# Low part of the weights first in each tile, with its buffers laid out for the preceding k tile

## The chip, the cores and the metric

The kernel runs on one core of a Trainium2 chip. The metric is the device time of one execution in microseconds. The core's TensorE (PE in the profile) does matrix products, VectorE (DVE), ScalarE (ACT) and GpSimd (POOL) do elementwise work, and SyncE (SP) issues most DMA transfers.

## The reference

A two-layer block over 256 tokens and 16 learned tokens (272 positions, width 1024), batch 1, all in float32. Cut to what matters for the change:

```python
for li in range(DEPTH):                                   # 2 layers
    h = h + mixer(rms_norm(h, norm_mix_g[li]), w_in[li], w_branch[li], w_out[li], ...)
    h = h + conv_ffn(rms_norm(h, norm_ffn_g[li]), w_ffn_in[li], ..., w_ffn_out[li], valid)
return rms_norm(h, norm_final_g)[:, PAD:]

def mixer(hn, w_in, w_branch, w_out, ...):
    proj = hn @ w_in                                      # 1024 x 13312
    # retention, HGRN2 and differential attention on slices of proj
    y_b = einsum('blnc,ncd->blnd', branches, w_branch)    # three times 1024 x 1024
    return sum(sigmoid(mg) * y_b, over n) @ w_out         # 1024 x 1024

def conv_ffn(hn, w_ffn_in, conv_w, conv_b, w_ffn_out, valid):
    u = hn @ w_ffn_in                                     # 1024 x 5632
    c = conv_b + sum(conv_w[j] * shifted(u, j))           # width 3
    gate, val = split(c, 2)
    return (silu(gate) * val) @ w_ffn_out                 # 2816 x 1024
```

## The kernel before, in words

All weights are cut into 128x128 tiles, 1,616 to a layer. They stand in memory in the order in which they are used, eight tiles to a chunk (404 chunks). For each chunk one DMA on SP's queue brings 512 KB into one of three buffers `wraw`. Products are made with about float32's precision from a faster matmul type: ACT copies the chunk to `whi`, rounded to that type, and DVE subtracts to get the rest, `wlo`. There are four buffers of each, each with room for 1,152 columns, 128 more than a chunk has. The activations are split the same way, into `xh` and `xl` (the first input projections and the ffn input), or into pairs of slots such as `b0hi`, `b0lo`, `yhi`, `ylo`, `ghi`, `glo`. A slot holds four k tiles of 272 positions one behind the other, so each k tile begins 1,088 bytes after the one before, which is 4 times 256 and 64 more.

For every weight tile `run` in `products` (lines 861 to 864) issues three matmuls that add into one PSUM bank: high weights with high activations, high weights with low activations, low weights with high activations. The weights are the stationary operand, so each matmul comes with a weight load; the activations move, 272 columns in layer 0 and in six kinds of product of layer 1 (those named in `FULL`), 258 in the other products of layer 1, which leave out the first 14 positions. A product covers two blocks of 128 output features (f = 0 and 1), each in its own PSUM bank, with k on the outside and f inside: (k 0, f 0), (k 0, f 1), (k 1, f 0) and so on. The first group has four blocks, those of `hq` 0 and 1, for its first four k tiles. Two products' results fit into PSUM at a time; DVE, ACT and POOL take them out while PE does the next product.

Exceptions are the last block of layer 0's ffn output, `("fo", 3)`, which does all k of f = 0 first and then those of f = 1, and the last layer's ffn output (`final`, lines 1340 on), in which the activations are stationary and 512 columns of weights move at a time.

Where a tile lies in its `whi` and `wlo` buffer is decided by `_places` (line 121): it wants each tile at a place modulo 256 bytes that is 64 times (k modulo 4), plus 96 for the 258-column products, plus 64 for those whose activations lie in slots (`BLOCK`). `whi` and `wlo` have the same places. `_runs` (line 146) turns the places of a chunk into one access pattern of evenly spaced runs, so that one ACT and one DVE instruction split a whole chunk. `_Weights.next` (line 568) hands out the tiles, and issues a new chunk's DMA and split when it comes to one; the split is due 6 us by the planner's clock (`LEAD`) before the first use.

The order of the instructions on each engine is set by a planner (`_Plan.order`) at build time. It simulates the engines with a cost for each operation and takes, on each engine, the operation that could start first, and among equals the one with the smallest due time (`key`). The three matmuls of a tile are one operation for it. The smaller matmuls of attention, retention and HGRN2 are put between the tiles in this way. Almost every ACT, DVE and POOL instruction carries line 549, the helper that records it; it is told apart by its tiles.

Of the kernel before, what the change touches and what calls it, by code (L numbers as in the profile page):

```python
# [36 lines left out]
CHUNK_TILES = 8  # L37
# [14 lines left out]
def _pairs(name, lo, hi):  # L52
# [34 lines left out]
def _turns(li):  # L87

    pairs = [x for x in ORDER if x[0][0] not in MARKS]
    if li == DEPTH - 1:
        pairs = [x for x in pairs if x[0] != "fo"]
    groups = [[x] for x in pairs]
    if li == 0:
        groups[:2] = [pairs[:2]]
    out = []
    for group in groups:
        if group == [("fo", 3)]:
            out.append([("fo", 3, k, f) for f in range(2) for k in range(FK)])  # L100
        else:
            nk = _ktiles(group[0][0])
            out.append([x + (k, f) for k in range(nk // 2) for x in group for f in range(2)])
            out[-1] += [x + (k, f) for x in group for k in range(nk // 2, nk) for f in range(2)]
    if li == DEPTH - 1:
        out.append([("fo", j, k, f) for k in range(FK) for j in range(KD // 2) for f in range(2)])
    return out
# [2 lines left out]
STREAM = sum(2 * _ktiles(n) for n, _ in ORDER if n[0] not in MARKS)  # L110


LINE = 256
APART = (0, 96)
BLOCK = 64
ROOM = CHUNK_TILES * P + 2 * LINE // 4
T0 = META - 2
FULL = ("rk", "rv", "hf", "hi", "dk", "dv")


def _places(depth=DEPTH):

    wants = []
    for li in range(depth):
        for name, j, k, _ in sum(_turns(li), []):
            if name == "fo" and (li == DEPTH - 1 or j == 3):
                wants.append(None)
                continue  # L130
            short = li == DEPTH - 1 and name not in FULL
            wants.append(APART[short] + BLOCK * (name[0] == "b" or name in ("wo", "fo")) + 64 * (k % 4))
    out = []
    for c in range(0, len(wants), CHUNK_TILES):
        at, places = 0, []
        for want in wants[c : c + CHUNK_TILES]:
            if want is not None:
                at += (want // 4 - at) % (LINE // 4)
            places.append(at)
            at += P  # L140
        assert at <= ROOM
        out.append(places)
    return out


def _runs(places):


    runs = []
    for i, at in enumerate(places):  # L150
        if runs and at == runs[-1][1] + runs[-1][2] * P:
            runs[-1][2] += 1
        else:
            runs.append([i, at, 1])
    out = []
    for i, at, n in runs:
        if out and out[-1][4] == n and (out[-1][3] == 1 or at == out[-1][1] + out[-1][2] * out[-1][3]):
            if out[-1][3] == 1:
                out[-1][2] = at - out[-1][1]
            out[-1][3] += 1  # L160
        else:
            out.append([i, at, 0, 1, n])
    return out


def _rope_perm(d):
# [387 lines left out]
class _Weights:  # L554
# [6 lines left out]
        self.used = 0  # L561
        self.places = _places()

    def part(self, t, at, step, runs, n):

        return bass.AP(t.tensor, t.offset + at, [list(t.ap[0]), [max(step, 1), runs], [1, n * P]])

    def next(self):
        c, i = divmod(self.used, CHUNK_TILES)
        self.used += 1  # L570
        if i == 0:
            due = self.plan.key
            room = [P, ROOM]
            raw = self.plan.tile(self.pool, [P, CHUNK_TILES * P], F32, "wraw", 3, f"wraw{c}")
            hi = self.plan.tile(self.pool, room, F32R, "whi", 4, f"whi{c}")
            lo = self.plan.tile(self.pool, room, F32R, "wlo", 4, f"wlo{c}")
            self.plan.key = due - LEAD
            pieces = 1 if c > 1 else 2
            for p in range(pieces):
                n = CHUNK_TILES // pieces  # L580
                cols = slice(p * n * P, (p + 1) * n * P)
                self.sp.dma_start(raw[:, cols], self.w[c][:, cols])
                for first, at, step, runs, each in _runs(self.places[c][p * n : (p + 1) * n]):
                    src = raw[:, (p * n + first) * P : (p * n + first + runs * each) * P].rearrange("p (r x) -> p r x", r=runs)
                    self.act.activation(self.part(hi, at, step, runs, each), src, AF.Copy)
                    self.dve.tensor_tensor(out=self.part(lo, at, step, runs, each), in0=src, in1=self.part(hi, at, step, runs, each).bitcast(F32), op=SUB)
            self.plan.key = due
            self.cut = hi, lo
        hi, lo = self.cut
        at = self.places[c][i]  # L590
        return hi[:, at : at + P], lo[:, at : at + P]

    def chunk(self):

        for _ in range(CHUNK_TILES):
            self.next()
        return self.cut


def build(tc, a, depth=DEPTH, probe=None):  # L600
# [7 lines left out]
def _trace(ctx, tc, plan, a, depth, probe):  # L608
    nc = tc.nc
# [8 lines left out]
    wp = ctx.enter_context(tc.tile_pool(name="wp", bufs=3))  # L618
# [222 lines left out]
    def products(xs, name, j, t0=0):  # L841

        if name in BASE or name == "fi":
            norm.next()
        if ahead:
            return ahead.pop()
        tiles = turns.pop(0)
        main = lambda: new(mp, [P, 2, 512], F32, "main", 2, "main")[:, :, t0:T]
        ps = {i: main() for i in sorted({x[1] for x in tiles})}
        to = {x: ps[x[0]][:, x[1], :] for x in {x[1::2] for x in tiles}}  # L850
        if (name, j) == ("fo", 3):

            to[j, 1] = main()[:, 1, :]
        cost = 3 * ((T - t0) / 2400 + 0.003)
        nk = _ktiles(name)
        for _, i, k, f in tiles:
            hi, lo = (x[:, t0:] for x in xs(k))
            plan.key = clock[0]
            wh, wl = weights.next()

            def run(o=to[i, f], wh=wh, wl=wl, hi=hi, lo=lo, first=k == 0, last=k == nk - 1):
                nc.tensor.matmul(o, wh, hi, start=first, stop=False)  # L862
                nc.tensor.matmul(o, wh, lo, start=False, stop=False)  # L863
                nc.tensor.matmul(o, wl, hi, start=False, stop=last)  # L864

            plan.main.append(plan.add("pe", run, cost, [to[i, f]], [wh, wl, hi, lo]))
            clock[0] += cost
        plan.key = clock[0] - 1.0
        if (name, j) == ("fo", 3):
            return [to[j, f] for f in range(2)]  # L870
        ahead.extend(ps[i] for i in ps if i != j)
        return ps[j]
# [64 lines left out]
    for li in range(depth):  # L937
        last = li == depth - 1
# [457 lines left out]
        for name, j in ORDER:  # L1396
# [4 lines left out]
            elif name in ("+hga", "+hgb"):  # L1401
                b = "ab".index(name[3])
# [3 lines left out]
            elif name in ("+daa", "+dab"):  # L1406
                b = "ab".index(name[3])
# [19 lines left out]
            both = slice(2 * j, 2 * j + 2)  # L1427
            if name in BASE:
                lo = 0 if name in FULL else t0
                ps = products(lambda k: x_tile(k, norm.folded), name, j, lo)  # L1430
# [16 lines left out]
                elif name in ("dq", "dk"):  # L1447
                    t = block(f"{name}{j // 2}")
# [3 lines left out]
                elif name == "rv":  # L1452
# [3 lines left out]
                    src = values(ps, st["rvt"][j // 2], (j % 2) * 2 * P)  # L1456
# [4 lines left out]
                elif name in ("hi", "dv"):  # L1461
                    n = name[0] + "v"
                    b = j // 2
# [5 lines left out]
                    src = values(ps, st[f"{n}t{b}"], (j % 2) * 2 * P)  # L1469
# [6 lines left out]
                else:  # L1476
                    t = block(f"{name}{j // 2}")
# [21 lines left out]
            elif name == "wo":  # L1499
                hi, lo = st["yhi"], st["ylo"]  # L1500
# [8 lines left out]
            elif name == "fi":  # L1509
# [25 lines left out]
            else:  # L1535
                hi, lo = st["ghi"], st["glo"]
# [14 lines left out]
                    norm.take(ks)  # L1551
        if not last:
            norm.finish()


# [16 lines left out]
```

## Time and profile before

| | us |
|---|---|
| Median of three runs | 1330.21 (1329.74 to 1330.99) |
| The profiled execution's own time | 1330.22 |
| Its span, first to last instruction | 1328.4 |
| PE busy | 1317.2 (99%) |
| DVE busy | 962.0 (72%) |
| ACT busy | 813.3 (61%) |

The profile is of one execution. A row of the costliest groups names line, engine, operation, the tile written and the tiles read, the shape and the count; then the busy time in us and the mean ns of one; then the idle time of the engine just before these instructions, and what ended most of it. PEld is PE's weight load, which runs beside its matmuls. Matmuls are pipelined: one is shown from its start to the end of its last result, so the matmuls of a stream overlap, and the distance from one start to the next says how fast PE goes. A row of the timeline has the start in us from the span's start, the duration, and the same names. In it, L862 is high weights with high activations, L863 high weights with low activations, and L864 low weights with high activations.

The chain of waits is followed back from the last instruction of the execution, at each step to what released it or to the instruction before it on its engine. In the table of waits a row gives the total idle time in us, how often, and the longest.

### The profile page before, as it was taken

How to read it: one execution, taken by the hardware profiler on the slowest of the kernel's cores; microseconds unless marked ns; L12 is line 12 of the kernel's file. 1: busy time of each engine (PE TensorE's matmuls, PEld its weight loads, DVE VectorE, ACT ScalarE, POOL GpSimd, SP SyncE). 2: the span in 40 equal slices, each digit the busy share in tenths (PEclk: the TensorE clock that was granted, in tenths of full speed). 3: DMA queues.
4: the chain of work that ended last, by engine and by line, in shares of the span. 5: the costliest groups of instructions: out<-in, count | busy, mean ns of one | idle time of the engine just before them, and what ended most of it. 6: DMA issues, size and time to landing. Idle time of an engine off the chain costs nothing.

```text
span 1328.4 us, 28916 instructions
## 1 busy us (share of the span) xinstructions
PE 1317.2 (99%) x11862; PEld 1288.8 (97%) x11862; DVE 962.0 (72%) x1630; ACT 813.3 (61%) x1372; POOL 83.6 (6%) x161
## 2 busy tenths in 40 slices
PE   9999999999999999999999999999999999999998
PEld 9999999999999999999999999999999999999986
DVE  7575777697576689886564757776985867898753
ACT  6747454746676567665446474557565775766643
POOL 5000000001010020000030000000011100200000
PEclk9999999999999999999999999999999999999999
DMA  7644543443544545555555445444445445465653
GB/s 270 193 142 153 167 161 128 143 143 128 179 139 159 175 159 175 182 170 187 177 173 179 158 157 163 160 136 144 141 153 175 141 160 198 138 208 189 199 184 109
DMA packets 60755, 219.07 MB, mean 165 GB/s; under 512 B 6864, under 2 KB 6992, under 8 KB 60624
## 3 DMA queue, kind: packets, MB, share of 16 engines
q1 hardware_dynamic: 60336, 216.71, 49.6%
q8 instruction: 93, 1.52, 0.5%
q10 hardware_dynamic: 288, 0.52, 0.1%
q14 instruction: 38, 0.31, 0.1%
HBM read 216.16 MB, written 1.05 MB: 164 GB/s over the span
## 4 chain that ended last, share of the span: by engine, by line
PE 94%; DVE 4%; issue 1%; ACT 0%; DMA 0%; SPq 0%; DVEq 0%
PE main L862 27%; PE main L864 27%; PE main L863 26%; PE fo L1372 2%; PE fo L1374 2%; PE fo L1373 2%; PE lev L1053 1%; DVE two_b L549 1%; PE ds L1237 1%; DVE wlo L549 1%; PE ms L549 1%; PE do L549 1%; PE ro L549 1%; PE ho L549 1%; PE vt L549 1%
## 5 line engine op out<-in xcount | busy, mean ns | idle before, releaser
L862 PE MATMUL main<-xh,whi 128*128 128x272 f32 (+1 forms) x2368 | 693.4, 293 | 0.3 <-issue 0.3
L864 PE MATMUL main<-xh,wlo 128*128 128x272 f32 (+1 forms) x2368 | 680.4, 287 | 0.7 <-DVE wlo L549 0.6
L863 PE MATMUL main<-xl,whi 128*128 128x272 f32 (+1 forms) x2368 | 671.7, 284 | 2.8 <-DVE xl L549 2.8
L549 DVE TENSOR_TENSOR wlo<-wraw,whi 128x1024 fp32r<-128x1024 f32 (+1 forms) x408 | 496.8, 1223 | 201.2 <-ACT whi L549 200.3
L549 ACT ACTIVATE whi<-wraw 128x1024 fp32r<-128x1024 f32 (+1 forms) x408 | 426.5, 1048 | 231.5 <-PE main L863 166.1
L863 PEld LDWEIGHTS main<-xl,whi 128*128 128x128 f32 x2368 | 448.9, 190 | 4.0 <-DVE xl L549 3.4
L862 PEld LDWEIGHTS main<-xh,whi 128*128 128x128 f32 x2368 | 445.6, 188 | 2.1 <-issue 0.4
L864 PEld LDWEIGHTS main<-xh,wlo 128*128 128x128 f32 x2368 | 444.6, 188 | 2.0 <-DVE wlo L549 2.0
L549 DVE SCALAR_TENSOR_TENSOR two_b<-main,small,two_b 128x256 f32<-128x256 f32 (+2 forms) x144 | 65.4, 487 | 29.1 <-ACT two_b L549 27.4
L549 ACT ACTIVATE two_b<-main,small 128x272 f32<-128x272 f32 (+1 forms) x72 | 37.3, 566 | 28.7 <-PE main L864 28.7
L549 POOL TENSOR_TENSOR y<-h,rstd 128x272 f32<-128x272 f32 x32 | 34.8, 1121 | 316.4 <-ACT rstd L549 316.4
L864 PE MATMUL main<-ghi,wlo 128*128 128x272 f32 x176 | 51.0, 290 | 0.0
L862 PE MATMUL main<-ghi,whi 128*128 128x272 f32 x176 | 50.9, 289 | 0.0
L863 PE MATMUL main<-glo,whi 128*128 128x272 f32 x176 | 50.2, 285 | 0.0
L549 ACT ACTIVATE vsrc<-main 128x544 f32<-128x544 f32 x24 | 15.0, 626 | 39.4 <-PE main L864 39.2
L862 PE MATMUL main<-b0hi,whi 128*128 128x272 f32 (+1 forms) x128 | 38.2, 298 | 0.0
L862 PE MATMUL main<-b1hi,whi 128*128 128x272 f32 (+1 forms) x128 | 38.1, 298 | 0.0
L864 PE MATMUL main<-yhi,wlo 128*128 128x272 f32 (+1 forms) x128 | 36.7, 286 | 0.0
L864 PE MATMUL main<-b2hi,wlo 128*128 128x272 f32 (+1 forms) x128 | 36.6, 286 | 0.0
L864 PE MATMUL main<-b1hi,wlo 128*128 128x272 f32 (+1 forms) x128 | 36.6, 286 | 0.0
L864 PE MATMUL main<-b0hi,wlo 128*128 128x272 f32 (+1 forms) x128 | 36.6, 286 | 0.0
L862 PE MATMUL main<-yhi,whi 128*128 128x272 f32 (+1 forms) x128 | 36.5, 285 | 0.0
(244 smaller groups left out, 1933.0 us busy)
## 6 DMA issues: line engine op xcount, KB each, us to landing
wraw<-in_w SPq DMA_DIRECT2D x402, 512.0 KB, 3.4
h<-in_h SPq DMA_DIRECT2D x4, 272.0 KB, 5.6
dec<-in_dec SPq DMA_DIRECT2D x2, 544.0 KB, 5.3
wraw<-in_w SPq DMA_DIRECT2D x4, 256.0 KB, 4.9
const<-in_const SPq DMA_DIRECT2D x1, 937.0 KB, 5.9
gain<-in_gl SPq DMA_DIRECT2D x1, 512.0 KB, 5.2
out<-y ACTq DMA_DIRECT2D x2, 256.0 KB, 2.8
out<-y SPq DMA_DIRECT2D x2, 256.0 KB, 2.7
```

Of the source, the lines that this page charges most:

```text
L549: self.plan.add(self.name, lambda: f(*args, **kw), cost, outs, ins, args[2] if method == "activation" else None)
L862: nc.tensor.matmul(o, wh, hi, start=first, stop=False)
L863: nc.tensor.matmul(o, wh, lo, start=False, stop=False)
L864: nc.tensor.matmul(o, wl, hi, start=False, stop=last)
L1053: nc.tensor.matmul(o, keys, x, start=True, stop=True)
L1237: nc.tensor.matmul(ss[m][:, at : at + nk], q[half, hd, q0 : q0 + P], k[half, hd, :nk], start=True, stop=True)
L1372: nc.tensor.matmul(o, gh, wh, start=False, stop=False)
L1373: nc.tensor.matmul(o, gl, wh, start=False, stop=False)
L1374: nc.tensor.matmul(o, gh, wl, start=False, stop=end)
```

## The change

In each tile the three passes are put in another order: low weights with high activations first, then high weights with high activations, then high weights with low activations. The first group of layer 0 keeps the old order. Within each pair of tiles of the same k the second block (f = 1) is now done before the first, except in `("fo", 3)`.

The places of `whi` and `wlo` are now worked out apart. A tile's high part lies at the place modulo 256 that belongs to its own k; its low part at the one of the tile that is used before it. In `wlo` the four tiles of f = 0 come first and then the four of f = 1, since with their places these fit the buffer in this order. Where they don't fit, the tiles lie one behind the other. `_grid` takes the place of `_runs`: an access pattern of two by four runs of 128 columns, where the places allow it; where not, the chunk is split in halves, with instructions of their own. `BLOCK` is gone; instead a tile of 48 columns (192 bytes) that nothing uses is added at the end to the pool of the weight buffers, ahead of the slots, which moves the slots by 192 bytes. In the last layer's ffn output a chunk's eight tiles stay together, at a place that depends on k.

```diff
 def _places(depth=DEPTH):
     wants = []
+    before = 0
     for li in range(depth):
-        for name, j, k, _ in sum(_turns(li), []):
-            if name == "fo" and (li == DEPTH - 1 or j == 3):
-                wants.append(None)
-                continue
-            short = li == DEPTH - 1 and name not in FULL
-            wants.append(APART[short] + BLOCK * (name[0] == "b" or name in ("wo", "fo")) + 64 * (k % 4))
+        tiles = sum(_turns(li), [])
+        for n in range(0, len(tiles), 2):
+            for i, (name, j, k, _) in reversed(list(enumerate(tiles[n : n + 2]))):
+                far = APART[li == DEPTH - 1 and name not in FULL]
+                at = 64 * (k % 4)
+                wants.append((far + at, far + before, li == DEPTH - 1 and name == "fo"))
+                before = at
+            wants[-2:] = wants[:-3:-1]
     out = []
     for c in range(0, len(wants), CHUNK_TILES):
...
+        chunk = wants[c : c + CHUNK_TILES]
+        if chunk[0][2]:
+            out.append([[chunk[0][0] // 4 + i * P for i in range(CHUNK_TILES)]] * 2)
+            continue
+        both = []
+        for n, order in ((0, range(CHUNK_TILES)), (1, [*range(0, CHUNK_TILES, 2), *range(1, CHUNK_TILES, 2)])):
+            at, places = 0, [0] * CHUNK_TILES
+            for i in order:
+                at += (chunk[i][n] // 4 - at) % (LINE // 4)
+                places[i] = at
+                at += P
+            both.append(places if at <= ROOM else [i * P for i in range(CHUNK_TILES)])
+        out.append(both)
     return out

+def _grid(places):
+    pairs = [places[i : i + 2] for i in range(0, len(places), 2)]
+    inside = pairs[0][1] - pairs[0][0]
+    step = pairs[1][0] - pairs[0][0] if len(pairs) > 1 else 2 * P
+    if all(x == [pairs[0][0] + i * step, pairs[0][0] + i * step + inside] for i, x in enumerate(pairs)):
+        return step, inside
+    return None
...
+    def split(self, raw, hi, lo, tiles):
+        at_hi, at_lo = ([x[i] for i in tiles] for x in self.places[raw[0]])
+        if not (_grid(at_hi) and _grid(at_lo)):
+            for n in (0, len(tiles) // 2):
+                self.split(raw, hi, lo, tiles[n : n + len(tiles) // 2])
+            return
+        src = self.part(raw[1], [i * P for i in tiles])
+        self.act.activation(self.part(hi, at_hi), src, AF.Copy)
+        self.dve.tensor_tensor(out=self.part(lo, at_lo), in0=src, in1=self.part(hi, at_hi).bitcast(F32), op=SUB)
...
+        swap = not _plain(name, j)
+        if swap:
+            tiles = [x for n in range(0, len(tiles), 2) for x in (tiles[n + 1], tiles[n])]
+        early = li == 0 and (name, j) == ORDER[0]
...
-            wh, wl = weights.next()
-
-            def run(o=to[i, f], wh=wh, wl=wl, hi=hi, lo=lo, first=k == 0, last=k == nk - 1):
-                nc.tensor.matmul(o, wh, hi, start=first, stop=False)
-                nc.tensor.matmul(o, wh, lo, start=False, stop=False)
-                nc.tensor.matmul(o, wl, hi, start=False, stop=last)
+            wh, wl = weights.next(swap)
+            passes = [(wh, hi), (wh, lo), (wl, hi)] if early else [(wl, hi), (wh, hi), (wh, lo)]
+
+            def run(o=to[i, f], passes=passes, first=k == 0, last=k == nk - 1):
+                for n, (w, x) in enumerate(passes):
+                    nc.tensor.matmul(o, w, x, start=first and n == 0, stop=last and n == 2)
...
         if not last:
             norm.finish()
+        else:
+            plan.tile(wp, [P, (LINE - 64) // 4], F32, "step", 1, "step")
```

More of the change, by code (lines that the diff above doesn't have):

```diff
@@ L114 @@
 APART = (0, 96)
-BLOCK = 64
 ROOM = CHUNK_TILES * P + 2 * LINE // 4
@@ L118, with _plain @@
 FULL = ("rk", "rv", "hf", "hi", "dk", "dv")
+def _plain(name, j):
+    return (name, j) == ("fo", 3)
 def _places(depth=DEPTH):
     wants = []
+    before = 0
     for li in range(depth):
-        for name, j, k, _ in sum(_turns(li), []):
-            if name == "fo" and (li == DEPTH - 1 or j == 3):
-                wants.append(None)
-                continue
-            short = li == DEPTH - 1 and name not in FULL
-            wants.append(APART[short] + BLOCK * (name[0] == "b" or name in ("wo", "fo")) + 64 * (k % 4))
+        tiles = sum(_turns(li), [])
[6 more added lines that the diff above has]
+            wants[-2:] = wants[:-3:-1]
@@ L133, in _places @@
     out = []
     for c in range(0, len(wants), CHUNK_TILES):
[L135 to L142, printed above, removed]
-    return out
[L146 to L163, printed above, removed]
+        chunk = wants[c : c + CHUNK_TILES]
@@ L562, in __init__, with part, next @@
         self.places = _places()
-    def part(self, t, at, step, runs, n):
-        return bass.AP(t.tensor, t.offset + at, [list(t.ap[0]), [max(step, 1), runs], [1, n * P]])
-    def next(self):
+    def part(self, t, places):
+        step, inside = _grid(places)
+        return bass.AP(t.tensor, t.offset + places[0], [list(t.ap[0]), [inside, 2], [step, len(places) // 2], [1, P]])
+    def split(self, raw, hi, lo, tiles):
[7 more added lines that the diff above has]
+        self.dve.tensor_tensor(out=self.part(lo, at_lo), in0=src, in1=self.part(hi, at_hi).bitcast(F32), op=SUB)
+    def next(self, swap=True):
         c, i = divmod(self.used, CHUNK_TILES)
@@ L582, in next @@
                 self.sp.dma_start(raw[:, cols], self.w[c][:, cols])
[L583 to L586, printed above, removed]
+                self.split((c, raw), hi, lo, range(p * n, (p + 1) * n))
             self.plan.key = due
             self.cut = hi, lo
-        hi, lo = self.cut
-        at = self.places[c][i]
-        return hi[:, at : at + P], lo[:, at : at + P]
+        i ^= swap
+        return tuple(t[:, x[i] : x[i] + P] for t, x in zip(self.cut, self.places[c]))
     def chunk(self):
@@ L596, in chunk @@
             self.next()
-        return self.cut
+        at = self.places[self.used // CHUNK_TILES - 1][0][0]
+        return tuple(t[:, at : at + CHUNK_TILES * P] for t in self.cut)
 def build(tc, a, depth=DEPTH, probe=None):
@@ L850, in products @@
         to = {x: ps[x[0]][:, x[1], :] for x in {x[1::2] for x in tiles}}
-        if (name, j) == ("fo", 3):
+        if _plain(name, j):
             to[j, 1] = main()[:, 1, :]
@@ L868, in products @@
         plan.key = clock[0] - 1.0
-        if (name, j) == ("fo", 3):
+        if _plain(name, j):
             return [to[j, f] for f in range(2)]
```

## The prediction

> **What bounds the kernel now.** I read the page first for the engine that sets the end, then the chain of waits, the waits of PE alone, and last the timeline, where the start times of neighbouring matmuls give the true step of PE. The page:
>
> ```profile
> span 1328.4 us, 28916 instructions
> ...
> PE 1317.2 (99%) x11862; PEld 1288.8 (97%) x11862; DVE 962.0 (72%) x1630; ACT 813.3 (61%) x1372; POOL 83.6 (6%) x161
> ...
> PE 94%; DVE 4%; issue 1%; ACT 0%; DMA 0%; SPq 0%; DVEq 0%
> ...
> L862 PE MATMUL main<-xh,whi 128*128 128x272 f32 (+1 forms) x2368 | 693.4, 293 | 0.3 <-issue 0.3
> L864 PE MATMUL main<-xh,wlo 128*128 128x272 f32 (+1 forms) x2368 | 680.4, 287 | 0.7 <-DVE wlo L549 0.6
> L863 PE MATMUL main<-xl,whi 128*128 128x272 f32 (+1 forms) x2368 | 671.7, 284 | 2.8 <-DVE xl L549 2.8
> ```
>
> PE is busy for 1317.2 of 1328.4 us, and the three passes of the main products have next to no idle time ahead of them (0.3, 0.7 and 2.8 us). The 284 to 293 ns per matmul overlap each other and are no step. The waits of PE say the same, in us in total, times, and the longest:
>
> ```profile
> PE main L863 <- DVE xl L549: 2.8, 3, 1.5
> ...
> PE main L864 <- DVE wlo L549: 0.6, 3, 0.2
> ```
>
> So no wait is to be removed; time can only come from the step between matmuls. The timeline gives it, in order: the low part's pass (L864), the two passes with the high part, and so on. The weight loads (PEld) of the same moments show that the load for the next matmul begins with the present one:
>
> ```profile
> 539.72 0.29 PE L862 MATMUL main<-xh,whi 128*128 128x272 f32 x1
> 539.84 0.28 PE L863 MATMUL main<-xl,whi 128*128 128x272 f32 x1
> 539.96 0.29 PE L864 MATMUL main<-xh,wlo 128*128 128x272 f32 x1
> ...
> 542.71 0.29 PE L862 MATMUL main<-xh,whi 128*128 128x272 f32 x1
> ```
>
> ```profile
> 539.84 0.19 PEld L864 LDWEIGHTS main<-xh,wlo 128*128 128x128 f32 x1
> 539.96 0.19 PEld L862 LDWEIGHTS main<-xh,whi 128*128 128x128 f32 x1
> ```
>
> From 539.72 to 542.71 lie 24 steps: 124.6 ns each. I call *offset* the byte at which the weights now being loaded begin, less the byte at which the present moving operand begins, modulo 256. In the layout of the built kernel before, xh and xl lie on multiples of 256, whi and wlo 64 past one, and a k tile moves both by 64. So a load that belongs to the k now moving has offset 64; the load of the next k's high part, which runs beside the last pass of every second tile, has 128. One in six is off.
>
> With the nanosecond starts of the trace, steps over 140 ns left out (276 steps, 64.5 us: other work or waits between), the 272-column matmuls step at 124.62 ns (5,570 steps). Two tiles in a row go 126, 120, 125, 127, 122, then 128 at the load that is off: 748 ns, hardly varying. The 258-column ones of layer 1, whose offset is 104 and each sixth time 168, step at 119.34 ns (3,092 steps), and have two patterns, seen at the same line 24 steps apart, 118.2 ns here:
>
> ```profile
> 1153.84 0.28 PE L862 MATMUL main<-xh,whi 128*128 128x258 f32 x1
> ...
> 1156.68 0.28 PE L862 MATMUL main<-xh,whi 128*128 128x258 f32 x1
> ```
>
> and 120.0 ns here:
>
> ```profile
> 1173.84 0.28 PE L862 MATMUL main<-xh,whi 128*128 128x258 f32 x1
> ...
> 1176.72 0.28 PE L862 MATMUL main<-xh,whi 128*128 128x258 f32 x1
> ```
>
> So a step depends on the steps before it: the same load at the same offset takes 116 or 122 ns.
>
> **The change, part by part.** *Order and layout.* Matmuls, loads and columns stay as many. With the low part first, the load beside the tile's third pass is the next tile's low part, and that lies where the present k's weights lie. Working the new layout through tile by tile with the slots on multiples of 256 (the 192-byte tile behind the weight buffers moves them from 64 to 0 past one), 5,800 of 5,904 loads beside 272-column matmuls have offset 64 (4,849 before), and 3,258 of 3,263 beside 258-column ones have 104 (2,721 before). What a chain of equal loads steps at is seen once before, in the first group, which has four tiles to a k: eleven equal loads in a row, 1.36 us from the first line to the last:
>
> ```profile
> 7.82 0.29 PE L862 MATMUL main<-xh,whi 128*128 128x272 f32 x1
> ...
> 9.18 0.29 PE L864 MATMUL main<-xh,wlo 128*128 128x272 f32 x1
> ```
>
> They are 126, 120, 125, 126, 123, 124, 123, 124, 122, 124, 123 ns: mean 123.6, the last six 123.3. Other such runs end at 123.1 to 124.0. I take 123.4, between them: (124.62 − 123.4) × 5,570 = 6.8 us less; the ends give 8.5 and 3.5 us less. For 258 columns the longest runs of equal loads are one that ends in 116, 122, 115, 116, 122, 116, 116 (its last eight 117.6) and one of eleven with mean 119.9; in the better pattern (122, 116, 122, 115, 116, then 118 off) the equal ones average 118.2. I take 118.4, nearest to that pattern: 0.94 × 3,092 = 2.9 us less; the ends give 5.4 less and 1.7 more.
>
> *The splits of the weights.* ACT's copy to whi and DVE's subtraction to wlo still handle 1,024 columns in one instruction for nearly all of the 404 chunks; by the layout some six more instructions on each engine are issued in all, three of them for the first two chunks. A 512-column ACT split took 0.52 us in the chain of the first 30 us; halving it adds the fixed part alone, an estimate of 0.1 to 0.2 us from the 1,048 ns of a 1,024-column one. The chain of the first 30 us runs through these, so I charge 0.5 us there (0 to 1.0). The runs of 128 instead of 256 columns I cost at nothing: DVE is busy 72% and ACT 61%, and the low part is ready 9 us (median over chunks) before its first use. Without that cover, each 0.1 us more per split would cost 40 us of DVE. The DMAs and their queue (SP) are unchanged.
>
> *The wait for the low part comes first.* wlo and hi are now wanted two steps, 0.25 us, earlier; behind that wait stand all later matmuls of PE's queue. The readiness of wlo falls short of 0.25 us only in chunks 0 to 3, which belong to the first group and keep the old order, and by 0.2 us in one later chunk: 0.2 us (0 to 0.5). The wait for xl moves to the tile's third pass, so each of its three waits can shrink by up to 0.12 us: nothing to 0.4 us less, taken as nothing, as what is late next is the same DVE.
>
> *Column order.* The second column block is done first, so its evacuation starts first; the product of about 6 us that follows, in the other of two PSUM buffers, hides this. Without it, one tile's 0.37 us would be paid in each of some 200 products.
>
> *The last product* (264 matmuls of 512 columns) gets a constant offset of 160 within a k tile. Before, its steps were 228.9 ns at offset 0, 232.6 at 64, 232.3 at 128, 228.9 at 192, mean 230.8. 160 lies between the last two: nothing, with ±0.7 us at the ends.
>
> *Tile without use, moved slots.* They issue nothing. The other matmuls that read slots shift against the constants; some two hundred are concerned, and at the 3 ns between best and worst offset seen above that is ±0.6 us.
>
> Sum: −6.8 − 2.9 + 0.5 + 0.2 = −9.0 us. The profiled execution took 1330.22 us (span 1328.4), the median of the three runs is 1330.21, so one stands for the other: 1321.2 us. With all ends together: 1314.6 to 1331.2 us.
>
> **The rivals.** *Steps add up by pass, and history doesn't matter.* Then each pass brings its row's mean: for 272 columns 124.9 (high load beside the low pass, same k), 125.9 and 122.0, together 372.8 against 374.1 now; for 258 columns 119.1, 119.6, 118.7, 357.3 against 358.1. That is 0.43 × 5,570 + 0.25 × 3,092 = 3.2 us less, with the 0.7 us of costs 1327.7 us. For it: the regular 126, 120, 125. Against it: the 116 or 122 ns of one and the same load, and 127 and 122 ns in the second tile where the first has 126 and 120 at equal offsets.
>
> *The load's place does nothing.* The 128 ns could belong to the step of the moving operand to a new k, which stays. Then only the 0.7 us remains: 1330.9 us. Against it: the last block of layer 0's ffn output, whose weights lie without regard to k and in which every tile has a new k, steps at 126.9 ns at offset 0, 125.2 at 64, 127.0 at 128 and 125.0 at 192. A rule of the Trainium skill (SBUF — State Buffer, "Who interferes with whom") speaks for this rival: TensorE has one read port for the moving operand and an independent one for weights, and never waits on another reader. By that rule the sum would be the 1330.9 us just given; the offsets' rows above do not agree with it.
>
> *Slower: equal loads lock into the slow rhythm.* A chain without the odd load need not settle where short runs point. If it held 126.0 ns (the mean beside the first pass now, at offset 64) and 120.0 ns (the slower pattern), it would cost 1.38 × 5,570 + 0.66 × 3,092 = 9.7 us, with the 0.7 us 1340.6 us. It decides from a step of 124.6 ns at 272 columns, with the other unchanged. For it: 119.9 ns in one run of eleven. Against: no run of equal loads at 272 columns ends above 124.0.
>
> *Better: they lock into the fast rhythm.* At 122.0 and 117.6 ns it would be 14.6 + 5.4 − 0.7 = 19.3 us less: 1310.9 us. Such steps occur, but singly.
>
> **How the numbers follow.** Chances: forecast 0.55 (its own range 1316 to 1326), steps by pass 0.15, no effect 0.08, slow rhythm 0.11, fast rhythm 0.11. The predicted time is 1321.2 us. The range of 1314 to 1331 us holds the first three cases and a little of the fast one, 0.8 in all. About 0.2%, 2.7 us, can be told from no change: above 1332.9 is slower, below 1327.5 faster. Faster: 0.55, the fast 0.11 and two fifths of the pass rival, which lies on that bound: 0.72. Same: its other 0.09 and 0.08: 0.17. Slower: 0.11.
>
> **What would show it.** In the timeline of layer 0's ffn input, 24 steps should take 2.96 us instead of 2.99, with no period of six; in layer 1's, 2.84 us in all stretches. PE's waits for wlo should stay under 1.5 us in total, and the split rows (1,048 and 1,223 ns) unchanged. The prediction is wrong if equal loads still step unequally, if the step is above 124.6 ns, or if splits lengthen so that wlo appears among the waits.

## The result and the profile after

The change makes the kernel slower: 1334.28 us (median of 8 runs, 1332.52 to 1337.94) against 1330.62 us for the kernel before in the same runs (1329.74 to 1332.48), a ratio of 1.0029 with a 95% interval of 1.0017 to 1.0041. I had forecast 1321.2 us, 1314 to 1331. The times also scatter more: 5.4 us between the extremes, 2.7 us before.

The page of the changed kernel, whose profiled execution took 1336.51 us. All three passes are now on line 881:

```profile
span 1334.7 us, 28930 instructions
...
PE 1323.3 (99%) x11862; PEld 1293.9 (97%) x11862; DVE 964.0 (72%) x1636; ACT 811.3 (61%) x1378; POOL 85.5 (6%) x161
...
PE 93%; DVE 4%; issue 1%; ACT 1%; DMA 0%; POOL 0%; SPq 0%; DVEq 0%; POOLq 0%
...
L881 PE MATMUL main<-xh,wlo 128*128 128x272 f32 (+1 forms) x2368 | 695.7, 294 | 3.3 <-DVE wlo L553 3.2
L881 PE MATMUL main<-xl,whi 128*128 128x272 f32 (+1 forms) x2368 | 678.9, 287 | 0.3 <-DVE xl L553 0.3
L881 PE MATMUL main<-xh,whi 128*128 128x272 f32 (+1 forms) x2368 | 677.5, 286 | 0.0
```

PE has as many matmuls as before, and is busy 6.1 us longer; DVE and ACT, with six more instructions each, are where they were. Its idle time ahead of the main passes is 3.6 us, as before (3.8 us), only the releaser has changed: the low weights are waited for 3.2 us instead of 0.6, xl 0.3 instead of 2.8. So nearly all of the 6.3 us of span lies in PE's step: 5.7 us by the table below. The timeline shows it. Two stretches of 24 steps in layer 0, between pass starts, 123.8 ns a step in the first (2.97 us) and 125.8 ns in the second (3.02 us):

```profile
40.56 0.28 PE L881 MATMUL main<-xh,wlo 128*128 128x272 f32 x1
...
43.53 0.28 PE L881 MATMUL main<-xh,wlo 128*128 128x272 f32 x1
```

```profile
20.99 0.29 PE L881 MATMUL main<-xh,wlo 128*128 128x272 f32 x1
...
24.01 0.29 PE L881 MATMUL main<-xh,wlo 128*128 128x272 f32 x1
```

And layer 1 with 258 columns, 121.3 ns a step (2.91 us); the two patterns of before were 118.2 and 120.0 ns:

```profile
681.96 0.29 PE L881 MATMUL main<-xh,wlo 128*128 128x258 f32 x1
...
684.87 0.29 PE L881 MATMUL main<-xh,wlo 128*128 128x258 f32 x1
```

The table counts steps under 140 ns between neighbouring main matmuls, from the nanosecond starts of the traces. "Six" is the time of the six matmuls on one k tile, with the values that occur most. The steps over 140 ns between neighbours of one width add up to 54.9 us in both kernels.

| | before | change |
|---|---|---|
| 272 columns: step, sum | 124.62 ns, 694.2 us | 124.80 ns, 695.4 us |
| six, most frequent | 748 and 749 ns (630 of 723) | 740 to 744 (301 of 717); 748 to 750 with 760 to 762 (375) |
| 258 columns: step, sum | 119.34 ns, 369.0 us | 120.61 ns, 372.7 us |
| six, most frequent | 708, 714 with 722 | 727 to 729 (242 of 427); 709 to 711 (55) |
| last product's step | 230.8 ns | 233.9 ns |

The times 748 to 750 and 760 to 762 of the changed kernel alternate: together they are one slow rhythm of twelve matmuls, 125.8 ns a step, beside a fast one of 740 to 744, 123.6 ns. By position, the changed kernel is 0.3 us later at its first product, 0.7 us at layer 1's beginning, 5.4 us near the end of the ffn input of layer 1, and 6.3 us after the last product.

### The profile page after: what moved, and what is told of

Same layout as the page of the kernel before. It is cut to its first block, busy times and chain, and to the rows that moved or that the text cites. A ratio compares the mean times of both kernels' runs of the same rounds, so it can differ in the third digit from the quotient of the medians.

```text
span 1334.7 us, 28930 instructions
## 1 busy us (share of the span) xinstructions
PE 1323.3 (99%) x11862; PEld 1293.9 (97%) x11862; DVE 964.0 (72%) x1636; ACT 811.3 (61%) x1378; POOL 85.5 (6%) x161
## 4 chain that ended last, share of the span: by engine, by line
PE 93%; DVE 4%; issue 1%; ACT 1%; DMA 0%; POOL 0%; SPq 0%; DVEq 0%; POOLq 0%
PE main L881 80%; PE fo L1390 2%; PE fo L1389 2%; PE fo L1391 2%; PE lev L1070 1%; DVE two_b L553 1%; DVE wlo L553 1%; PE ds L1254 1%; PE do L553 1%; PE ms L553 1%; PE ro L553 1%; PE ho L553 1%; DVE xl L553 1%; PE vt L553 1%; PE s L553 0%
## 5 line engine op out<-in xcount | busy, mean ns | idle before, releaser
L881 PE MATMUL main<-xh,wlo 128*128 128x272 f32 (+1 forms) x2368 | 695.7, 294 | 3.3 <-DVE wlo L553 3.2
L881 PE MATMUL main<-xl,whi 128*128 128x272 f32 (+1 forms) x2368 | 678.9, 287 | 0.3 <-DVE xl L553 0.3
L881 PE MATMUL main<-xh,whi 128*128 128x272 f32 (+1 forms) x2368 | 677.5, 286 | 0.0
L553 DVE TENSOR_TENSOR wlo<-wraw,whi 128x1024 fp32r<-128x1024 f32 (+2 forms) x414 | 497.3, 1208 | 207.0 <-ACT whi L553 205.7
L553 ACT ACTIVATE whi<-wraw 128x1024 fp32r<-128x1024 f32 (+2 forms) x414 | 426.8, 1034 | 239.3 <-PE main L881 174.4
L553 ACT ACTIVATE two_b<-two_b 128x272 f32<-128x272 f32 (+1 forms) x44 | 18.6, 423 | 32.3 <-DVE two_b L553 32.3
L553 POOL COPY tails<-vsrc 128x32 f32<-128x32 f32 x32 | 10.8, 352 | 423.8 <-ACT vsrc L553 370.8
L881 PE MATMUL main<-b2hi,whi 128*128 128x272 f32 (+1 forms) x128 | 36.6, 286 | 0.0
L881 PE MATMUL main<-ylo,whi 128*128 128x272 f32 (+1 forms) x128 | 36.5, 285 | 0.0
```

The costliest lines, as they stand in the source:

```text
L553: self.plan.add(self.name, lambda: f(*args, **kw), cost, outs, ins, args[2] if method == "activation" else None)
L881: nc.tensor.matmul(o, w, x, start=first and n == 0, stop=last and n == 2)
```

## The experiments

My theories after the result were two. The first: a load is disturbed by the present moving operand and also by the next one, so that the change only moves the odd distance (the low part of a new k, laid out for the old one, lies at distance 0 instead of 64 to the operand it will meet). The second: a stream of matmuls has several rhythms that keep themselves up, and what came before decides which one it falls into. The rival: other engines' work beside PE, or the order of passes, makes the slow steps.

**Streams alone.** The block's computation is left out, and PE repeats four kinds of stream with nothing beside it. "Place" below is the first number of a tile's place modulo 256, as in `APART`; the offset is that number plus 64 at 272 columns and plus 8 at 258. These streams lie at places 0 and 96, as in the kernels; the core of the edit is the generator of the operands' starts (in columns):

```diff
+        mov = k * T + t0 if step else t0
+        at = own + (k * (T + 0) if step else 0)
+        low = own + (last * T if step else 0)
+        for i, f in enumerate((0, 1) if kind == "old" else (1, 0)):
+            wl = at
+            if kind == "new" and i == 0:
+                wl = low
+            hh, hl, lh = (mov, at, 0, 0, f), (mov, at, 1, 0, f), (mov, wl, 0, 1, f)
+            out += [hh, hl, lh] if kind == "old" else [lh, hh, hl]
```

> This kernel leaves the block's computation out: PE alone runs long streams of 144 matmuls on fixed data, each after one small fp32 matmul of a different width (eight widths), with the places of x and of the weights as in the kernels. Four kinds of stream: old (order and places of before), new (order and places of the change), order (new order, low part at the place of its own k), even (old order, k step of 1,088 bytes left out, so that all operands keep one distance). 272 columns at offset 64 and 258 columns at offset 104; then other offsets. Theory 1, a load is disturbed by the present moving operand and by the next one, and the change moves the odd distance from the one to the other: new steps no faster than old (124.6 and 119.3 ns), even steps at 123.4 ns or less with all six steps equal. Theory 2, a stream has several rhythms that each keep themselves up, and the small matmul before it decides which: the eight starts of one kind fall into groups, new at 272 columns into 123.6, 124.9 and 125.9 ns, at 258 columns into 118.3 and 121.4 ns, old at 272 columns into one at 124.7 ns. Rival, the slower steps come from other engines' work beside PE: here, without it, new steps at the forecast 123.4 and 118.4 ns whatever the start.

Mean steps in ns of the eight starts, once settled:

| stream | 272 columns | 258 columns |
|---|---|---|
| old | 124.7 (eight) | 118.1 (one), 119.7 (seven) |
| order | 124.7 (eight) | 118.1 (three), 119.7 (five) |
| new | 123.6 (seven), 125.8 (one) | 121.4 (three), 119.9 (five) |
| even | 123.3 (eight) | 117.8 (three), 121.1 (five) |

The timeline of the even streams at 258 columns, in which all loads have the very same distance to their operands, after two different starts: 24 steps in 2.83 us (118 ns) and in 2.91 us (121 ns):

```profile
650.65 0.28 PE L372 MATMUL main<-xh,wh 128*128 128x258 f32 x1
...
653.48 0.28 PE L372 MATMUL main<-xh,wh 128*128 128x258 f32 x1
...
790.02 0.28 PE L372 MATMUL main<-xh,wh 128*128 128x258 f32 x1
...
792.93 0.28 PE L372 MATMUL main<-xh,wh 128*128 128x258 f32 x1
```

and the new streams at 272 columns, 2.96 us and 3.02 us:

```profile
37.81 0.28 PE L372 MATMUL main<-xh,wl 128*128 128x272 f32 x1
...
40.77 0.28 PE L372 MATMUL main<-xh,wl 128*128 128x272 f32 x1
...
399.76 0.29 PE L372 MATMUL main<-xh,wl 128*128 128x272 f32 x1
...
402.78 0.29 PE L372 MATMUL main<-xh,wl 128*128 128x272 f32 x1
```

With nothing beside PE the kernels' rhythms come out to a tenth of a nanosecond (six times 124.7 is 748, six times 125.8 is 755, the mean of 749 and 761). So the rival falls for the rhythms: other work is not needed for them. The order alone brings no new rhythm: its streams have those of old. The second theory holds, and more strongly than I had put it: even loads that are all alike have two rhythms at 258 columns. Of the first theory only a part stands: new is slower than even, and at this place no new stream at 258 columns reaches 118 ns. That it is the next operand which disturbs is not shown, since even leaves out the operands' k step as well.

At 258 columns three kinds split at the same starts: behind small matmuls of 16, 24 and 48 columns order and even are in their fast rhythm and new is at 121.4 ns, behind the five wider ones it is the reverse; old is fast behind 16 columns alone. So the start sorts these streams, and not chance from one stream to the next.

**The change once more.** The same kernel, a second profile:

> The changed kernel unaltered, for a second profile. Theory 2 (the rhythm is chosen anew after each interruption): the step of layer 0's products falls into the same rhythms, about 741, 749 and 761 ns for six matmuls, but in other shares than in the first profile of the change, and the time differs by more than 1 us from 1336.5 us. Theory 1 alone, and the rival of other engines' work, with one rhythm for one pattern: the same shares within a few per cent at the same places, and a time within 1 us of 1336.5 us.

It took 1334.66 us. At 272 columns 69% of the sixes were in the fast rhythm and 25% in the slow one, against 42% and 52% in the first profile: a step of 124.32 ns, and 3.2 us less in the sum of these steps. At 258 columns nothing moved (120.57 ns). With 1.4 us more in the steps over 140 ns, that is the 1.9 us between the two times. The granted clock is no rival here: it is 1.00 over the products in both profiles.

But the rhythm is not drawn anew all over layer 0. Compared six by six, 475 of the 670 that are in one of the two rhythms in both profiles are in the same one, at the same place of the program. Of the other 195, 20 lie near the start (13 to 37 us), and 175 in one stretch from 508 to 643 us. In that stretch, the same 24 steps took 3.02 us in the first profile and 2.96 us in this one:

```profile
549.95 0.29 PE L881 MATMUL main<-xh,wlo 128*128 128x272 f32 x1
...
552.97 0.29 PE L881 MATMUL main<-xh,wlo 128*128 128x272 f32 x1
```

```profile
549.90 0.28 PE L881 MATMUL main<-xh,wlo 128*128 128x272 f32 x1
...
552.86 0.28 PE L881 MATMUL main<-xh,wlo 128*128 128x272 f32 x1
```

So most places take the same rhythm each time, and one long stretch that takes the other makes a difference of some 2 us.

**The order without the layout.** The low part goes first, but lies at the place of its own k:

```diff
-                wants.append((far + at, far + before, li == DEPTH - 1 and name == "fo"))
+                wants.append((far + at, far + at, li == DEPTH - 1 and name == "fo"))
...
-        for n, order in ((0, range(CHUNK_TILES)), (1, [*range(0, CHUNK_TILES, 2), *range(1, CHUNK_TILES, 2)])):
+        for n, order in ((0, range(CHUNK_TILES)), (1, range(CHUNK_TILES))):
```

> The change without its layout: low part first and second block first, but the low part lies at the place of its own k, as the high part. Theory 1: this has the odd distance to the present operand, one load in six at 128, and none to the next, as before; the six matmuls take 748 ns, and the time is that of before plus at most 1 us, 1331 us. If the new layout of the change is harmless and the new order alone is slow, it is 1334 us or more with the pairs of the change (741, 749, 761 and, at 258 columns, 728 ns). If the odd load costs what was forecast, it is 6 to 10 us slower than the change, 1341 us or more.

1332.50 us, ratio to before 1.0020 (1.0010 to 1.0029). The six matmuls take 748 or 749 ns again in 631 of 718 cases, the step at 272 columns is 124.62 ns as before, and at 258 columns 119.58 ns. Order, swapped blocks, moved slots and the last product's new place, which this kernel keeps, therefore cost about 2.5 us and bring no new rhythm. Of the profile's 2.4 us, 0.8 are the last product (233.9 ns here too), 0.7 the larger share of the slower pattern at 258 columns; the rest is in steps over 140 ns. The other 1.8 us to the change's 1334.28 would be the layout's, on the wrong side, but the two ratios' intervals overlap. The steps show its part more firmly: 1.0 ns, 3.2 us, at 258 columns, and at 272 between 1.0 us more and 1.7 us less by the two profiles of the change.

**All places.** Streams in the new order and places for each place of the weights in steps of 8 bytes, with six starts, some of the old, and the last product's form:

```diff
+    for cols, t0 in ((258, 14), (272, 0)):
+        for kind, by, reps in (("new", 2, 6), ("old", 4, 4)):
+            for own in range(0, 64, by):
```

> The block's computation is left out again: streams of 96 matmuls on fixed data, each after one small fp32 matmul, for every place of the weights in steps of 8 bytes (new order and places) or 16 bytes (old), six and four starts each, at 258 and 272 columns; and the last product's form, 512 columns of weights moving, at 16 distances. If a rhythm depends on the place and on the start (theory 2): new at 258 columns and place 96 stays at 119.9 or 121.4 ns, there is a band of places around 224 (118.1 ns in the first stream run on both starts) where all six starts give at most 118.5 ns, and at 272 columns place 0 gives 123.6 ns for most starts and 125.8 ns for the others. The last product's form is slower by 3 ns a step at the distance of the change, 160, than at the mean of 64, 128, 192 and 0. If the order alone or other work is what slows the change (rival), the place moves nothing: all places within 1 ns at 258 columns, and no difference in the last form.

A selection:

| columns, stream | place: step in ns, of all starts |
|---|---|
| 258, new | 72: 118.1; 88: 118.1; **96: 119.9 to 121.4**; 104: 120.3; 120: 129.2; 160: 121.4; 176: 117.0 or 118.1; 224: 118.1 |
| 272, new | **0: 123.6 (four) or 125.8 (two)**; 8: 125.8 or 126.9; 88: 128.1; 120: 123.6; 216: 124.7 |
| 272, old | 0: 124.7; 224: 126.9; 240: 124.2 |
| last product's form, by distance | 240 and 0: 226.7; 160: 233.3; seven others also 233.3; 176: 230.0 |

The places of the kernels are in bold. Eight bytes next to 96, at 88, the new streams are at 118.1 ns from every start; at 120 they are at 129.2. What I had called equal, offsets that are all the same, says nothing until one says which offset. Here the weights alone move, so place and distance change together. The kernel before speaks for the distance: its products from x and those from slots have their weights 64 bytes apart, but at the same distance to the operand, and in both most sixes at 272 columns take 748 or 749 ns (487 of 550 and 144 of 185).

The rule that I weighed (Trainium skill, SBUF — State Buffer, "Who interferes with whom") is that TensorE's two read ports are independent and that PE never waits on anyone. A load's place without effect, as I read it in my rival, is not what these rows show: moving the weights alone by 32 bytes takes the step from 118.1 to 129.2 ns. Whether the ports have to do with it, no run shows. A small regularity, which was not followed up: several of the times of six matmuls lie multiples of about 3.3 ns apart (708.3, 715, 718.3, 721.7 and 728.3 at 258 columns; 741.7, 748.3, 751.7, 755 and 761.7 at 272), though not all (706.7 and 740.0 in the even streams).

**One place in the change.** The place of the 258-column products, 88 instead of 96, so their offset is 96 instead of 104. The last product's weights move by the same 8 bytes:

```diff
-APART = (0, 96)
+APART = (0, 88)
```

> The change with one number altered: the place of the weights of the 258-column products is 88 instead of 96, so their offset is 96 instead of 104, one and the same for all loads as before. If the slow rhythm at 258 columns comes from the place (theory 2): steps at 118.1 ns instead of 120.6, 3,090 steps, so 7.8 us less than the change: 1326.5 us, and faster than before. If equal loads are what counts and the exact place doesn't, or if the loss is in other work: within 1 us of the change, 1334 us.

1328.32 us, ratio to before 0.9989 (0.9979 to 0.9998), 6.0 us less than the change, where I expected 7.8. Steps at 258 columns fell to 118.36 ns, 2.25 ns or 6.9 us less than in the change, and the last product's to 233.5 ns, 0.1 us; the sixes are 705 and 711 or 712 ns. The timeline, the same products as shown above for the change, 24 steps in 2.84 us:

```profile
681.27 0.28 PE L881 MATMUL main<-xh,wlo 128*128 128x258 f32 x1
...
684.11 0.28 PE L881 MATMUL main<-xh,wlo 128*128 128x258 f32 x1
```

This settles where the change loses in layer 1: with the same order, and with a layout that differs in nothing but these 8 bytes, the place decides.

**Three places.** The places that six starts had shown as the best for each form (120 and 88 in the streams' count, since the tile `shift` adds 64 bytes to both numbers):

```diff
-APART = (0, 96)
+APART = (56, 24)
...
+    fixed([P, 16], "shift")
...
-            out.append([[chunk[0][0] // 4 + i * P for i in range(CHUNK_TILES)]] * 2)
+            out.append([[(chunk[0][0] - APART[1] - 64) % LINE // 4 + i * P for i in range(CHUNK_TILES)]] * 2)
...
-            plan.tile(wp, [P, (LINE - 64) // 4], F32, "step", 1, "step")
+            plan.tile(wp, [P, (LINE - 128) // 4], F32, "step", 1, "step")
```

> The change with three places altered, by the streams: weights of 272-column products at offset 184 (123.6 ns from all six starts), of 258-column ones at offset 96 (118.1 ns from all six), and the last product's operands at distance 0 (226.7 instead of 233.3 ns). Theory 2: from the change's 1334.3 us, 0.9 ns on 5,570 steps, 2.5 ns on 3,090 and 6.4 ns on 264 are 5.0, 7.7 and 1.7 us less: 1320 us, with less scatter between executions than the change. If the kernel's interruptions or other engines' work decide the rhythm whatever the place: 1330 us or more.

1329.49 us, ratio 0.9997 (0.9987 to 1.0006): 9.5 us short of what I expected. 258 columns were right (118.35 ns), the last product half right (230.1 ns, not 226.7), but 272 columns stepped at 125.24 ns: 171 sixes of 716 in the fast rhythm at 741 or 742 ns, 239 at 748 or 749, 239 at 761 or 762, the two halves of the slow rhythm. Six starts had been too few.

**The old order at its best places.** The kernel before with nothing but its two places altered:

```diff
-APART = (0, 96)
+APART = (240, 176)
```

> The kernel before with its own order and layout, and only the two places altered to the best that the streams show for it: 240 at 272 columns (124.2 instead of 124.7 ns), 176 at 258 columns (118.1 or 119.7 instead of 119.3 ns). Theory 2: 2.5 and 2.6 us less than before, 1325 us, and slower than the change with its best places. If the place matters only together with the new order: 1330 us as before. If the odd load in six costs what was forecast, no place brings it below 1328 us.

1332.56 us, ratio 1.0021 (1.0011 to 1.0031), where I expected 1325: at 272 columns 124.96 ns, part of the sixes near 744 as in the streams but others at 768, a rhythm that four starts had not shown. At 258 columns 119.09 ns, the two rhythms 708 and 718. Four starts showed neither all the rhythms nor how often a kernel falls into each.

**More starts.** The new streams with 24 starts at ten places; one, two or three small matmuls stand ahead:

```diff
+                for j in range(1 + rep // 8):
+                    n = JOLT[(rep + j) % 8] + 4 * (rep // 8)
+                    at = 16 * ((rep + 3 * j) % 16)
+                    nc.tensor.matmul(bank[:, :n], raw[:, at : at + 128], raw[:, 512 + 8 * rep : 512 + 8 * rep + n], start=True, stop=True)
```

> The block's computation is left out: streams of 96 matmuls in the new order and places, with 24 different starts (one, two or three small fp32 matmuls of different widths and operands ahead) at five places for 258 and five for 272 columns. Theory 2, the rhythm is chosen by the start, and six starts were too few: at place 120 and 272 columns a second and third rhythm appear beside 123.6 ns, near 124.9 and 126.9 ns, as in the kernel that used it; at place 0 the same three in other shares; at place 88 and 258 columns 117.5 and 118.5 ns. Rival, other engines' writes or the kernel's own waits make the slow rhythms at place 120: all 24 starts at 123.6 ns.

At 272 columns, place 120, which had seemed safe, gave 123.6 ns 14 times and 125.8 ns 10 times; place 0 gave 123.6 17 times and 125.8 seven times. At 258 columns, place 96 gave 119.8 to 121.4 in all 24 and never 118, place 88 118.0 or 118.1 in all. Place 224, at 118.1 from six starts, gave 119.1 to 119.3 ns in 11 of the 24. So the start alone brings the slow rhythm at place 120, without other engines' work; the rivals that need such work fall here too. In the slow streams at place 120 the sixes alternate, 748 or 749 ns and 761 or 762, as they do in the kernel with three places: its sixes at 748 belong to this slow rhythm and are no third one. What the small matmul does is not fixed by its width alone: with the same six widths as in the streams at all places, place 0 at 272 columns gave the same again (125.8 ns at the first and fifth start), but place 96 at 258 columns did not.

**A version that beats both.** The change with place 88 and the last product's operands at distance 0; 272 columns stay as in the change:

```diff
-APART = (0, 96)
+APART = (0, 88)
...
-            out.append([[chunk[0][0] // 4 + i * P for i in range(CHUNK_TILES)]] * 2)
+            out.append([[(chunk[0][0] - APART[1]) // 4 + i * P for i in range(CHUNK_TILES)]] * 2)
```

> The change with place 88 for the 258-column products and the last product's operands at distance 0. Theory 2: as with place 88 alone (1328.3 us), and the last product's 264 steps at 230.1 ns, as the kernel with three altered places had them, instead of 233.5: 0.9 us less, 1327.4 us, 0.2% faster than before. If the last product's gain is given back at the end of the kernel, where other engines finish: 1328.3 us.

1327.12 us (11 runs, 1326.35 to 1327.54), ratio to before 0.9977 (0.9968 to 0.9986): faster than both kernels, and with less scatter. Its page, and 96 steps of the last product, 22.10 us or 230.2 ns each:

```profile
span 1325.2 us, 28930 instructions
...
PE 1313.2 (99%) x11862; PEld 1284.5 (97%) x11862; DVE 963.9 (73%) x1636; ACT 811.6 (61%) x1378; POOL 85.5 (6%) x161
```

```profile
1261.72 0.39 PE L1390 MATMUL fo<-whi,glo 128*128 128x512 f32 x1
...
1283.82 0.39 PE L1390 MATMUL fo<-whi,glo 128*128 128x512 f32 x1
```

In the change the same count takes 22.47 us, 234.1 ns each:

```profile
1267.73 0.39 PE L1391 MATMUL fo<-wlo,ghi 128*128 128x512 f32 x1
...
1290.20 0.40 PE L1391 MATMUL fo<-wlo,ghi 128*128 128x512 f32 x1
```

Against the kernel with place 88 the last product gave 0.85 us of the 1.2 us.

## Why the prediction was wrong, point by point

- *What bounds the kernel* was right: time changed almost only with PE's step, and the waits ahead of the main passes kept their sum.
- *The layout* came out as worked out: in the built program 5,796 loads beside 272-column matmuls have offset 64 and 3,255 beside 258-column ones 104.
- *What a chain of equal loads steps at* is the step that failed. I took one settled value from a few short runs. At 272 columns the value, 123.4 ns, was that of one rhythm (123.6 ns); a second one at 125.8 ns takes a quarter to a half of the sixes, and the mean is 124.3 to 124.8 ns: 1.7 us less to 1.0 us more in place of 6.8 us less. The sign that I had named, 24 steps of layer 0's ffn input in 2.96 us, was there in the second profile and not in the first (3.02 us). The 123.3 ns at which my eleven loads ended is the even stream's step, from all eight starts; the change's loads lie at one distance to the operand that moves beside them, but not to the one that they will meet. At 258 columns I took 118.4 ns; the streams show 119.8 to 121.4 ns for this place from 24 starts, and the kernel 120.6 ns: 3.7 us more in place of 2.9 us less. My upper bound there, 119.9 ns from one run of eleven, lay below it. I had seen two patterns for one layout in the profile before and still forecast a single value for the new one.
- That *the place counts only through being equal* was implied and false. "Equal" left out which value it is, as the kernel with place 88 shows (6.0 us). It also left out the load's distance to the next operand, which the change makes odd (0 instead of 64 at 272 columns); that this does harm is not shown by itself, but fits: at 258 columns, place 96, even streams have a rhythm at 117.8 ns, new ones none below 119.8 ns.
- *The rivals.* The slow rhythm came nearest in its mechanism: 120.0 ns was its number at 258 columns (120.6 measured), while at 272 columns it had 126.0 against a mixture, so that its time, 1340.6 us, was 6 us too long. It had a chance of 0.11. Steps adding up by pass, without history, is refuted by the new streams, in which one sequence of loads takes 123.6 or 125.8 ns; the load's place doing nothing by the streams at all places, although its 1330.9 us lay nearer to the measured time than the forecast and every other rival's.
- *The splits* were right: the first product starts 0.3 us later (0.5 charged), and the rows of ACT and DVE keep their busy time (426.8 and 497.3 us, 426.5 and 496.8 before); six more, shorter instructions in each take the means from 1,048 to 1,034 and from 1,223 to 1,208 ns.
- *The wait for the low part* was mis-sized: 3.2 us in all, 2.6 us more, where I charged 0.2 and named 1.5 in total as a sign of being wrong. It came out in the sum because xl's 2.8 us became 0.3, which I had taken as nothing; that DVE is late next in either case I had named.
- *The last product* was mis-sized: 0.8 us more, just outside ±0.7. I interpolated between the steps at distances 128 and 192, and the steps do not run smoothly with the distance (233.3 ns at 160).

## What to carry to other kernels

A step of PE that changed regularly under one and the same load was here the sign of rhythms that keep themselves up: measure the whole stream, from many starts, before taking a short run's mean for its settled value. Where a layout is to make loads alike, the value at which they are alike must be scanned afterwards; here 8 bytes turned a loss of 0.3% into a gain of 0.1%. Streams alone, from enough starts, tell which rhythms exist, but only the kernel tells how often each is taken, and two profiles of it are to be compared stretch by stretch.

## What I had not expected of the hardware

One and the same sequence of matmuls and operands runs at 117.8 or 121.1 ns a step for as long as it was followed (144 matmuls), depending on what ran ahead of it. The step at 258 columns ranges from 117.0 to 129.2 ns over places 8 bytes apart. And an execution's share of the slow rhythm varied between two profiles of one program, 52% and 25% of the sixes, nearly all of it in one stretch of 135 us. What in the machine makes the rhythms was not found: the runs show that they need neither other engines nor a change of order, and nothing more.
